# Earlier raw weight loads, an output weight in quarters, and a third projection bank in a hybrid decoder layer

## The chip, the core and the metric

The kernel runs on one core of a Trainium2 chip. A core has a matrix engine (TensorE, PE in the profile), a vector engine (VectorE, DVE), a scalar engine (ScalarE, ACT), GpSimd (POOL) and SyncE (SP), which here issues all DMA transfers. The engines run side by side, each through its own instructions in order, and wait for one another by semaphores. The metric is the device time of one execution in microseconds (us), the median of several runs.

## What is computed

One decoder layer for 1024 tokens of width 1024, in float32. Cut to what matters here:

```python
u = rmsnorm(h, mix_pre_norm)
z = u @ w_in                                   # 48 column tiles of 128
o_attn = dilated_attention_branch(z_attn)      # three groups, rotary q and k
o_rwkv = rwkv7_time_mix(z_rwkv, ...)           # a delta-rule recurrence over the tokens
gate_attn, gate_rwkv = split(sigmoid(z_gate))
merged = gate_attn * (o_attn @ w_attn_up) + gate_rwkv * (o_rwkv @ w_rwkv_up)
h = h + rmsnorm(merged @ w_out, mix_post_norm)
f = square(relu(rmsnorm(h, ffn_pre_norm) @ w_ff_in)) @ w_ff_out
h = h + rmsnorm(f, ffn_post_norm)
h = h + rmsnorm((p @ w_ple) * sigmoid(h @ w_ple_gate), ple_post_norm)
```

Every large product is made of three matmuls on operands that are split into a high and a low part (hi x hi, hi x lo, lo x hi; lines 310, 312 and 314).

## The kernel before

**Order.** The program is written out by a planner (`Order`, line 141) that keeps a clock `sch.t` of its own, an estimate of where PE stands. Two kinds of work are mixed. *Chains* are generators for everything with dependencies (the RWKV recurrence, attention, evacuations); each says when it wants to go on. The *dense list* (`dense`) holds large matmul tiles that fill PE while the chains wait. An entry has a gate (a condition), a load and a body. `pick` (line 186) takes the first entry whose gate is open; an entry without a gate is taken only when it is first. `fill` (line 197) starts a tile; before it goes on, it runs every *job* that is still pending and then calls `ahead`, which picks the following tile and issues its load. So a tile's weight is fetched while the tile before it runs.

**Jobs.** `soon(t, job)` (line 175) puts a job off to the planner's estimate of a landing, plus 0.2 us. The split of a raw weight into high and low part is such a job.

**Weights.** `wload` (line 331) takes a raw tile `wr` of 128 x 1024, starts its DMA (512 KB), and splits it: ACT copies it to `wh`, POOL subtracts twice to get `wl`. `wr`, `wh` and `wl` have two buffers each. The loads of the RWKV output (`load_or`, line 271) and the quarters of the output weight (`wsplit`, line 341) use the same two `wr` buffers.

**Who keeps whose order.** PE runs in written order throughout. While the recurrence runs (until the last `post` is done), ACT, DVE, POOL and SP do too. During attention only SP does; after it, in the merges, SP doesn't either, and the framework's scheduler orders these engines.

**Stages that matter here.** The projection tiles come in units: r, k and v for the recurrence (four units), then q, k and v for attention (six), with 16 gate tiles among and behind them. A tile has two halves of 24 matmuls of 512 tokens (`add_z`, line 490; `zhalf`, line 367). Each half fills one PSUM bank, taken by `zbank` (line 360) in turn from z0, z1 and, outside the recurrence, s0. The evacuation of a half of r, k or v is an ACT copy and a DVE operation that adds the token shift; of q or k an ACT copy, after the second half four DMA swaps of 32 rows (`sw`) and the rotary product on POOL and DVE.

In the recurrence, `invert` (line 708) solves the triangular blocks of one unit by 31 steps of small DVE operations and ends with transposes (line 739 is the first of these); `fold` (line 790) then combines the blocks. Its transposes "at" (line 801) and the scan (line 851) use the banks s0 and s1.

After attention come eight merges (`merge`, line 1282). Each loads its weight (384 KB) and two gate rows `g`, makes 24 matmuls from the RWKV output (`bk`) and 12 from the attention output (`z`), multiplies both by the gates on DVE, and splits the sum into `mt`. Merge 1 also fetches the first half of the output weight: `wo_half(0, GA)` at line 1301, four quarters of 512 KB, each split by ACT and DVE. The output projection (`out_0`, line 1366) reads it after merge 7.

Of the kernel before, what the change touches and what calls it, by code (L numbers as in the profile page):

```python
# [10 lines left out]
F32 = mybir.dt.float32  # L11
F32R = mybir.dt.float32r
AF = mybir.ActivationFunctionType
OP = mybir.AluOpType
# [12 lines left out]
NU = RW // 128  # L27
# [113 lines left out]
class Order:  # L141
# [4 lines left out]
    def __init__(self):  # L146
        self.t = self.dep = 0.0
        self.exact = False
        self.chains = []
        self.jobs = []  # L150
        self.dense = []
        self.cur = self.nxt = None
        self.busy = {}
        self.form = None
        self.held = None
        self.kept = []
        self.written = Written()
# [11 lines left out]
        self.chains.append([self.t + after, prio, gen])  # L169
        self.chains.sort(key=lambda c: c[1])  # L170

    def add(self, body, load=None, gate=None, late=False):
        self.dense.append((gate, load, body, late))

    def soon(self, t, job):

# [6 lines left out]
        self.jobs.append(jobs)  # L183
        self.spawn(due(), 0)

    def pick(self):
        for i, (gate, load, body, late) in enumerate(self.dense):
            if gate() if gate else i == 0:
                del self.dense[i]
                return body(*load()) if load else body(), late  # L190
        return None

    def ahead(self):
        if self.nxt is None:
# [23 lines left out]
        return d > 0  # L218

    def run(self):  # L220
        while self.chains or self.cur or self.dense or self.nxt:
            self.let_go(self.t)
            for c in self.chains:
                if c[0] <= self.t:
                    try:
                        self.dep = self.t
                        d = next(c[2])
                        c[0] = self.dep + LAG if d is None else self.t + d
                    except StopIteration:
                        self.chains.remove(c)  # L230
                    break
            else:
                if not self.fill():
                    self.t = max(self.t + 0.1, min((c[0] for c in self.chains), default=0.0))
                    assert self.t < 1e4
# [27 lines left out]
def layer(ctx: ExitStack, tc: tile.TileContext, x, pT, wz, wup, w_out, wff1, w_ff2, w_ple, w_pleg,  # L263
# [3 lines left out]
    sch = Order()  # L267
# [54 lines left out]
    def wait(cond):  # L322
        while not cond():
            yield 0.1
# [3 lines left out]
        yield from sch.free(tag)  # L328
        return psum.tile(shape, F32, name=name, tag=tag), tag

    def wload(src, n=1024):
        raw = wpool.tile([128, 1024], F32, name="wr")
        land = SY.dma_start(raw[:, :n], src)
        hi = wpool.tile([128, 1024], F32R, name="wh")
        lo = wpool.tile([128, 1024], F32R, name="wl")

        def split():
            S.activation(hi[:, :n], raw[:, :n], AF.Copy)
            for c in (slice(0, n // 2), slice(n // 2, n)):
                G.tensor_tensor(lo[:, c], raw[:, c], hi[:, c], OP.subtract)  # L340
        if ("X", 0) in done:
            sch.soon(land, split)
        else:
            split()
        return hi, lo
# [9 lines left out]
    upool = ust.enter_context(tc.tile_pool(name="u", bufs=1, side="right"))  # L355
    uT = [[upool.tile([128, KT, 512], F32R, name=f"u{p}{h}") for h in range(2)] for p in "hl"]

    zn = [0]

    def zbank():  # L360
        tags = ("z0", "z1", "s0")
        if ("X", 0) in done and ("P", NU - 1, 1) not in done:
            tags = tags[0:2]
        zn[0] += 1
        return psum.tile([128, 512], F32, name="z", tag=tags[zn[0] % len(tags)])

    def zhalf(ps, hi, lo, h):
# [122 lines left out]
    def add_z(wi, evac, gate=None):  # L490
        def body(hi, lo):
            for h in range(2):
                ps = zbank()
                yield from zhalf(ps, hi, lo, h)
                evac(h, ps)
                sch.let_go()
        sch.add(body, lambda: wload(wz[wi]), gate)

    def add_gate(j):
        def evac(h, ps):  # L500
# [207 lines left out]
    def invert(w):  # L708
# [29 lines left out]
        q, q2 = slice(0, 32), slice(32, 64)  # L738
        V.transpose(TN[q, :, q].rearrange("s q p -> s p q"), X[q].rearrange("q t p -> q p t"))
        d0 = V.end  # L740
        yield max(V.end - LEAD - sch.t, 0.0)
        V.transpose(TA[q2, :, :, q2].rearrange("p c h t -> p t c h"),
                    X[q2].rearrange("q t (c h) -> q t c h", h=2))
# [46 lines left out]
    def fold(w):  # L790
        d = U[w]
        AR, BK, TM, TN, UV, wc = (d[n] for n in ("AR", "BK", "TM", "TN", "UV", "wc"))
        for b in range(4):
# [3 lines left out]
            S.activation(TM[:, 4 * b:4 * b + 4, 0], ps.rearrange("p c (h k) -> p c h k", h=2), AF.Copy)  # L797
            sch.hold(tag)
        t0 = sch.dep
        for b in range(2):  # L800
            ps, tag = yield from chain_bank([128, 4, 128], "at", ("s0", "s1"))
            for i in range(4):
                c = 8 * b + 2 * i
                tr(ps[:, i, :], AR[:, 0, c:c + 2].rearrange("p c t -> p (c t)"), 0.11)
            for i in range(2):
                S.activation(BK[0:64, 8 * b + i:8 * b + 8:2, :], ps[64 * i:64 * i + 64], AF.Copy)
            sch.hold(tag)
# [472 lines left out]
        orT[w] = (hl[:, 0], hl[:, 1])  # L1280

    def merge(j):
        def load():
            hi, lo = wload(wup[j], 768)
            if j % 2 == 0:
                gt = [rtile([128, T], "g", t) for t in ("a", "kk")]
            else:
                gt2 = rtile([128, 2, T], "g", "BT")
                gt = [gt2[:, 0], gt2[:, 1]]
            for n in range(2):  # L1290
                land = SY.dma_start(gt[n], g_scr[2 * j + n])

            def gates():
                for g in gt:
                    S.activation(g, g, AF.Sigmoid)
            sch.soon(land, gates)
            return hi, lo, gt

        def body(hi, lo, gt):
            if j == 1:  # L1300
                wo[0] = wo_half(0, GA)
            ga, gr = gt
            wk = [(hi[:, i * 128:(i + 1) * 128], lo[:, i * 128:(i + 1) * 128]) for i in range(6)]
            def second(hs):
                ps = bank(("s1", "s2") if j < 2 else ("s1", "s2", "m0", "m1"))
                yield from mm3(ps, [wk[2 + i] + (orT[i][0][:, hs], orT[i][1][:, hs]) for i in range(NU)])
                V.tensor_tensor(gr[:, hs], gr[:, hs], ps, OP.mult)

            for hs in halves if j < 7 else ():
                yield from second(hs)  # L1310
            for h, hs in enumerate(halves):
                if j == 7:
                    yield from second(hs)
                while ("A", h) not in done or sch.t < OA_t[h]:
                    yield 0.0
                if mT[0][h] is None:
                    for p in range(2):
                        mT[p][h] = mtile("hl"[p], h, [128, KT, 512], f"mt{p}{h}", F32R)
                ps = zbank()
                yield from mm3(ps, [wk[i] + (oh[:, hs], ol[:, hs]) for i, (oh, ol) in enumerate(oaT)])  # L1320
                V.tensor_tensor(ga[:, hs], ga[:, hs], ps, OP.mult)
                V.tensor_tensor(ga[:, hs], ga[:, hs], gr[:, hs], OP.add)
                S.activation(mT[0][h][:, j, :], ga[:, hs], AF.Copy)
                V.tensor_tensor(mT[1][h][:, j, :], ga[:, hs], mT[0][h][:, j, :], OP.subtract)
        sch.add(body, load, lambda: ("B", 5) in done)

    for j in range(8):
        merge(j)
# [20 lines left out]
    def wo_half(c, tags):  # L1349
# [6 lines left out]
            res += [(hi[:, k, :], lo[:, k, :]) for k in range(2)]  # L1356
        return res

    def tok(i):
        return i // 4, slice((i % 4) * 128, (i % 4) * 128 + 128)  # L1360

    wo = {}
    y0 = {}
    ss0 = const.tile([128, 8], F32, name="ss0")

# [880 lines left out]
```

## Time and profile before

| | |
|---|---|
| median of 3 runs | 1735.56 us (1735.06 to 1738.82) |
| the profiled execution, its own time | 1735.81 us |
| its span, first to last instruction | 1733.8 us |
| mean granted clock of PE | 0.994 |
| HBM read, written | 196.50 MB, 81.79 MB |
| DMA issues of raw projection weights (`wr<-in_wz_dram`) | 48 of 512 KB, median 4.8 us to landing |

How to read the profile: a group is named by line, engine and operation, output <- inputs by the program's names. Operations that go through the planner's helper all have line 118, so the names tell them apart. In a timeline, a line gives start, duration, engine, line, operation, names, shape and count; in brackets stands the idle time of the engine just before, and what ended it. PE's matmuls overlap, so one shows some 0.39 us while they start about 0.23 us apart. The granted clock is a share of full speed. "SPq" are the DMA issues of SP; a transfer lands later.

### The profile page before, as it was taken

The numbers are of one execution on the slowest core, as the hardware profiler recorded it, in microseconds if no ns is written. First come the engines' busy times: TensorE is split into PE (matmuls) and PEld (weight loads), VectorE is DVE, ScalarE is ACT, GpSimd is POOL, SyncE is SP. The second block draws the span as 40 slices with busy tenths as digits, with TensorE's granted clock in tenths as the row PEclk, the third lists the DMA queues.
The fourth block names the chain that finished last, engine by engine and source line by source line (L and its number), as shares of the span: only waits on it lengthen the run. The fifth ranks groups of instructions, "written<-read, shape, count | busy, mean of one in ns | idle before, by whom it ended". The sixth has DMA issues, their size and how long they took to land.

```text
span 1733.8 us, 26821 instructions
## 1 busy us (share of the span) xinstructions
PE 1705.6 (98%) x10048; PEld 1394.3 (80%) x10048; DVE 1169.8 (67%) x2066; ACT 755.6 (44%) x1391; POOL 684.4 (39%) x491
## 2 busy tenths in 40 slices
PE   9999999999999999999899999999999999999998
PEld 8877888887887777776688888788888888888887
DVE  6377778677645666674664753688888888887644
ACT  5823334241425555444443465543443443443354
POOL 1222121120232323233240135877777777772311
PEclk9999999999999999999999999999999999999999
DMA  4621221221325866665642259466566566567611
GB/s 166 216 85 37 68 80 56 92 74 62 111 62 183 275 214 231 216 224 181 231 173 98 79 200 355 155 221 217 189 221 221 189 219 224 189 229 266 209 49 49
DMA packets 111491, 286.73 MB, mean 165 GB/s; under 512 B 12673, under 2 KB 13057, under 8 KB 110850
## 3 DMA queue, kind: packets, MB, share of 16 engines
q1 hardware_dynamic: 111362, 285.03, 47.7%
q8 instruction: 79, 1.29, 0.3%
q14 instruction: 50, 0.41, 0.1%
HBM read 196.50 MB, written 81.79 MB: 161 GB/s over the span
## 4 chain that ended last, share of the span: by engine, by line
PE 51%; DVE 2%; DMA 1%; ACT 1%; issue 1%; POOL 0%; SPq 0%; DVEq 0%; ACTq 0%; POOLq 0%
PE bk L314 9%; PE bk L310 9%; PE bk L312 9%; PE z L314 7%; PE z L310 7%; PE z L312 7%; PE tp L301 1%; DMA wr<-in_wz_dram 1%; DVE hh L118 0%; DMA wr<-in_w_out_dram 0%; ACT SB L118 0%; DMA g<-gscr 0%; PE cb L293 0%; DMA wr<-oscr 0%; DVE tot L118 0%
## 5 line engine op out<-in xcount | busy, mean ns | idle before, releaser
L118 POOL TENSOR_TENSOR wl<-wr,wh 128x512 fp32r<-128x512 f32 (+1 forms) x112 | 158.8, 1439 | 510.5 <-ACT wh L118 497.2
L310 PE MATMUL z<-uh,wh 128*128 128x512 f32 (+1 forms) x800 | 313.9, 392 | 6.6 <-DVE v L118 2.7
L314 PE MATMUL z<-uh,wl 128*128 128x512 f32 (+1 forms) x800 | 314.2, 393 | 1.8 <-POOL wl L118 1.8
L312 PE MATMUL z<-ul,wh 128*128 128x512 f32 (+1 forms) x800 | 313.0, 391 | 1.3 <-DVE ul L118 1.3
L118 DVE TENSOR_TENSOR tot<-tot,bk 128x512 f32<-128x512 f32 x417 | 273.0, 682 | 54.8 <-PE bk L314 54.7
L310 PEld LDWEIGHTS z<-uh,wh 128*128 128x128 f32 x800 | 151.6, 189 | 38.7 <-ACT wh L118 5.9
L314 PEld LDWEIGHTS z<-uh,wl 128*128 128x128 f32 x800 | 151.4, 189 | 34.2 <-issue 3.9
L312 PEld LDWEIGHTS z<-ul,wh 128*128 128x128 f32 x800 | 151.3, 189 | 31.4 <-issue 2.8
L310 PE MATMUL bk<-duo 128*128 128x512 f32 x420 | 163.5, 389 | 0.2 <-DVE hr L118 0.2
L314 PE MATMUL bk<-duo 128*128 128x512 f32 x420 | 163.4, 389 | 0.0
L312 PE MATMUL bk<-duo 128*128 128x512 f32 x420 | 163.4, 389 | 0.0
L118 ACT ACTIVATE wh<-wr 128x1024 fp32r<-128x1024 f32 (+2 forms) x94 | 81.0, 862 | 101.0 <-DMA wr<-in_wz_dram 46.6
L118 ACT ACTIVATE hr<-hr 128x512 f32<-128x512 f32 x96 | 60.7, 633 | 129.3 <-DVE hr L118 127.8
L118 POOL TENSOR_TENSOR duo<-sum,duo 128x512 fp32r<-128x512 f32 x60 | 84.1, 1401 | 51.5 <-ACT duo L118 51.5
L310 PEld LDWEIGHTS bk<-duo 128*128 128x128 f32 x420 | 78.8, 188 | 16.9 <-ACT wl L118 0.6
L312 PEld LDWEIGHTS bk<-duo 128*128 128x128 f32 x420 | 78.8, 188 | 16.4
L314 PEld LDWEIGHTS bk<-duo 128*128 128x128 f32 x420 | 78.8, 188 | 16.3
L118 DVE TENSOR_TENSOR hr<-hr,z 128x512 f32<-128x512 f32 x80 | 54.8, 685 | 52.2 <-PE z L314 50.5
L118 POOL TENSOR_TENSOR sw<-sw,rope 128x1024 f32<-128x1024 f32 x12 | 36.5, 3043 | 135.3 <-DMA sw<-qk 104.0
L118 ACT ACTIVATE duo<-sum 128x512 fp32r<-128x512 f32 x68 | 42.6, 628 | 108.1 <-DVE sum L118 106.4
L310 PE MATMUL z<-f,wh 128*128 128x512 f32 x212 | 82.6, 390 | 0.7 <-ACT pa L118 0.7
L312 PE MATMUL z<-f,wh 128*128 128x512 f32 x212 | 82.5, 389 | 0.0
(368 smaller groups left out, 3864.1 us busy)
## 6 DMA issues: line engine op xcount, KB each, us to landing
duo<-bs SPq DMA_DIRECT2D x60, 512.0 KB, 4.1
wr<-in_wz_dram SPq DMA_DIRECT2D x48, 512.0 KB, 4.8
bs<-OTB SPq DMA_DIRECT2D x35, 512.0 KB, 5.9
w2r<-in_w_ff_dram SPq DMA_DIRECT2D x32, 512.0 KB, 5.3
wr<-in_wff_dram SPq DMA_DIRECT2D x56, 256.0 KB, 3.6
w2e<-in_w_ff_dram SPq DMA_DIRECT2D x26, 512.0 KB, 6.1
bs<-duo SPq DMA_DIRECT2D x25, 512.0 KB, 6.4
hr<-p1scr SPq DMA_DIRECT2D x48, 256.0 KB, 3.1
```

The source lines that it names most:

```text
L118: return f(*a, **kw)
L301: PE.transpose(out_, a, ident if idn is None else idn)
L310: PE.matmul(ps, ah, bh, start=start and i == 0, stop=False, skip_group_check=not start)
L312: PE.matmul(ps, ah, bl, start=False, stop=False, skip_group_check=not start)
L314: PE.matmul(ps, al, bh, start=False, stop=i == n - 1, skip_group_check=not start)
```

## The change

Three edits in one.

1. *Raw weights half a tile sooner.* Entries of the dense list get a fifth field `raw`, a function that takes a raw tile and starts its DMA. After the first half of a projection tile (once the recurrence is over) and after the first half of a merge's second loop, `raw_ahead` looks at the dense list. If the first entry is the one that would be picked, has such a function, and no job is pending, it is taken off the list and its raw DMA is issued. The next `pick` then uses it: its split is put off to a landing that by then is near or past.
2. *The output weight's quarters.* `wo_half(0, GA)` in merge 1 becomes `wo_part(0)` to `wo_part(3)` in merges 1 to 4. Each fetches one quarter; its split is a job instead of being issued at once.
3. *A third projection bank up to the first fold.* `zbank` keeps s0 in turn until `invert` of the first unit has issued its first transpose ("fold"), instead of giving it up when the recurrence starts. `zin` holds the bank of the half that isn't evacuated yet; `fold` waits until that isn't s0 before it uses s0.

```diff
@@ class Order
-    def add(self, body, load=None, gate=None, late=False):
-        self.dense.append((gate, load, body, late))
+    def add(self, body, load=None, gate=None, late=False, raw=None):
+        self.dense.append((gate, load, body, late, raw))
...
+    def which(self):
+        return next((i for i, d in enumerate(self.dense) if (d[0]() if d[0] else i == 0)), None)
+
     def pick(self):
-        for i, (gate, load, body, late) in enumerate(self.dense):
-            if gate() if gate else i == 0:
-                del self.dense[i]
-                return body(*load()) if load else body(), late
-        return None
+        if self.raw:
+            (_, load, body, late, _), got = self.raw
+            self.raw = None
+            return body(*load(got)), late
+        i = self.which()
+        if i is None:
+            return None
+        _, load, body, late, raw = self.dense.pop(i)
+        return body(*(load(raw()) if raw else load())) if load else body(), late
+
+    def raw_ahead(self):
+        i = self.which()
+        if i == 0 and not self.raw and not any(self.jobs) and self.dense[i][4]:
+            d = self.dense.pop(i)
+            self.raw = d, d[4]()
...
-    def wload(src, n=1024):
+    def wraw(src, n=1024):
         raw = wpool.tile([128, 1024], F32, name="wr")
-        land = SY.dma_start(raw[:, :n], src)
+        return raw, SY.dma_start(raw[:, :n], src)
+
+    def wload(src, n=1024, got=None):
+        raw, land = got or wraw(src, n)
...
-    zn = [0]
+    zn, zin = [0], set()
 
     def zbank():
         tags = ("z0", "z1", "s0")
-        if ("X", 0) in done and ("P", NU - 1, 1) not in done:
+        if "fold" in done and ("P", NU - 1, 1) not in done:
             tags = tags[0:2]
         zn[0] += 1
+        zin.clear()
+        zin.add(tags[zn[0] % len(tags)])
...
@@ add_z, body
                 evac(h, ps)
+                zin.clear()
                 sch.let_go()
-        sch.add(body, lambda: wload(wz[wi]), gate)
+                if h == 0 and ("P", NU - 1, 1) in done:
+                    sch.raw_ahead()
+        sch.add(body, lambda got: wload(wz[wi], got=got), gate, raw=lambda: wraw(wz[wi]))
@@ invert, after the first transpose to TN
+        done.add("fold")
@@ fold, before the transposes "at"
+        yield from wait(lambda: "s0" not in zin)
@@ merge
-        def load():
-            hi, lo = wload(wup[j], 768)
+        def load(got):
+            hi, lo = wload(wup[j], 768, got)
...
-            if j == 1:
-                wo[0] = wo_half(0, GA)
+            if j in (1, 2, 3, 4):
+                wo_part(j - 1)
...
+                if h == 0:
+                    sch.raw_ahead()
-        sch.add(body, load, lambda: ("B", 5) in done)
+        sch.add(body, load, lambda: ("B", 5) in done, raw=lambda: wraw(wup[j], 768))
...
+    def wo_part(i):
+        if i == 0:
+            parts[:] = pieces(GA, "wo0", F32R)
+            wo[0] = []
+        raw = wpool.tile([128, 1024], F32, name="wr")
+        land = SY.dma_start(k2(raw), w_out[256 * i:256 * i + 256, halves[0]].rearrange("(k p) c -> p k c", p=128))
+        hi, lo = parts[i], parts[4 + i]
+
+        def split():
+            S.activation(hi, raw, AF.Copy)
+            V.tensor_tensor(lo, raw, hi, OP.subtract)
+        sch.soon(land, split)
+        wo[0] += [(k2(hi)[:, k, :], k2(lo)[:, k, :]) for k in range(2)]
```

More of the change, by code (lines that the diff above doesn't have):

```diff
@@ L151, in __init__ @@
         self.dense = []
-        self.cur = self.nxt = None
+        self.cur = self.nxt = self.raw = None
         self.busy = {}
@@ L220, in run @@
     def run(self):
-        while self.chains or self.cur or self.dense or self.nxt:
+        while self.chains or self.cur or self.dense or self.nxt or self.raw:
             self.let_go(self.t)
@@ L1357, in wo_half @@
         return res
+    def wo_part(i):
[10 more added lines that the diff above has]
+        wo[0] += [(k2(hi)[:, k, :], k2(lo)[:, k, :]) for k in range(2)]
     def tok(i):
         return i // 4, slice((i % 4) * 128, (i % 4) * 128 + 128)
-    wo = {}
+    wo, parts = {}, []
     y0 = {}
```

## The prediction

> **What bounds the kernel now.** I read the page first. TensorE (PE) sets the time, and none of the changed lines removes a matmul.
>
> ```profile
> span 1733.8 us, 26821 instructions
> ...
> PE 1705.6 (98%) x10048; PEld 1394.3 (80%) x10048; DVE 1169.8 (67%) x2066; ACT 755.6 (44%) x1391; POOL 684.4 (39%) x491
> ```
>
> PE is idle for 1733.8 - 1705.6 = 28.2 us. No edit can gain much more than those gaps and whatever else they cost. The waits of PE come next: who ended its idle time, total, times, longest.
>
> ```profile
> PE bk L310 <- ACT wh L118: 5.6, 1, 5.6
> PE z L310 <- DVE v L118: 2.7, 1, 2.7
> PE z L310 <- ACT wh L118: 2.0, 1, 2.0
> ...
> PE pt L301 <- ACT SB L118: 1.3, 2, 0.9
> ...
> PE rc L301 <- DVE row L118: 1.1, 1, 1.1
> ```
>
> The first three stand out, and each belongs to one part of the change. To see whether a gap costs more than its idle time, I asked for windows behind each and two undisturbed ones (columns: window, its length, busy time of the five engines, granted PE clock, DMA share, GB/s).
>
> ```profile
> 148.00:154.00 6.00, 4.35 (x12) 3.51 (x13) 5.93 (x11) 0.64 (x1) 3.66 (x3) 0.72 0.00 0
> 612.00:622.00 10.00, 8.46 (x30) 6.04 (x31) 6.24 (x15) 6.12 (x16) 2.95 (x2) 0.66 0.66 240
> 852.00:858.00 6.00, 4.83 (x14) 3.44 (x15) 1.53 (x3) 3.27 (x5) 3.46 (x4) 0.63 0.62 221
> 863.00:896.00 33.00, 33.00 (x147) 27.35 (x146) 23.49 (x32) 14.84 (x20) 11.54 (x9) 1.00 0.46 162
> ...
> 1200.00:1250.00 50.00, 50.00 (x222) 41.42 (x221) 42.65 (x61) 17.31 (x30) 39.67 (x30) 1.00 0.63 213
> ```
>
> Behind each gap the clock falls, while an undisturbed stretch of merges has 1.00. The lost clock is 6 x 0.28 = 1.68 us in the first window. In the second it is 10 x 0.34 = 3.4, less some 0.1 that falls on idle time, so 3.3. In the third it is 6 x 0.37 = 2.22, less half of the 1.17 us that were idle, so 1.63. The gaps therefore cost their idle time and 6.6 us more.
>
> [...]
>
> **Part by part: the third projection bank.** Each projection half (24 matmuls) fills one PSUM bank. With two banks, a half waits for the evacuation of the half two before it.
>
> ```profile
> 95.23 0.47 PE L310 MATMUL z<-uh,wh 128*128 128x512 f32 x1 [0.70 <-ACT gst L118]
> 149.65 0.53 PE L310 MATMUL z<-uh,wh 128*128 128x512 f32 x1 [2.67 <-DVE v L118]
> ...
> 94.35 0.74 DVE L118 SCALAR_TENSOR_TENSOR v<-z,pr,v 128x511 f32<-128x511 f32 x1
> ...
> 148.77 0.73 DVE L118 SCALAR_TENSOR_TENSOR v<-z,pr,v 128x511 f32<-128x511 f32 x1
> ...
> 154.98 0.74 DVE L118 SCALAR_TENSOR_TENSOR v<-z,pr,v 128x511 f32<-128x511 f32 x1
> ```
>
> The second gap ends 0.15 us after the DVE operation on v is done (149.50); DVE sat in the inverse's many small operations. The first gap ends 0.14 us after the v operation at 94.35 (95.09), so I read it as the same wait although the row names gst. With three banks both halves find a bank that was emptied long before. What is late next: the half starts at 149.65 - 2.67 = 146.98 and takes 24 x 33.00 / 147 = 5.4 us. The next needs the bank freed at 149.50 and starts near 152.4; the one after it needs the bank freed at 155.72 and starts near 157.8. Neither waits. Gain: 0.70 + 2.67 + 1.68 = **5.05 us**.
>
> The edit adds a wait: the fold's transposes "at" stand back while a projection sits in s0. Behind them in the same chain are the scan and the read-out. By counting banks from the start (six taken before this stage, then two per tile), the half that DVE leaves in the row below is the 26th and the last in s0; the next goes to z1, used two halves earlier and free.
>
> ```profile
> 197.44 0.73 DVE L118 SCALAR_TENSOR_TENSOR k<-z,pr,k 128x511 f32<-128x511 f32 x1
> ...
> 198.23 1.04 PE L301 MATMUL at<-cs,AR 128*128 128x128 f32 x8
> ```
>
> DVE leaves that half's bank at 198.17, the transposes start at 198.23. With the 0.15 us hop seen above they are at most some 0.1 late. Bounds: nothing, and 0.7 us (the gap at 95.23) if the order shifts. I take 0.2, near the rows.
>
> **Raw weight half a tile sooner.** A tile's raw weight (512 KB) is fetched at the start of the tile before. There, SP has four swaps of q or k ahead of it, and these wait for the evacuation.
>
> ```profile
> 601.20 2.41 SPq L137 DMA_DIRECT2D sw<-qk  x4
> 603.71 0.53 SPq L137 DMA_DIRECT2D wr<-in_wz_dram  x1
> ...
> DMA to landing us min/median/max: 4.6/4.8/5.0
> ...
> 610.95 1.06 ACT L118 ACTIVATE v<-z 128x512 f32<-128x512 f32 x1 [3.89 <-PE z L314]
> 611.82 1.05 ACT L118 ACTIVATE wh<-wr 128x1024 fp32r<-128x1024 f32 x1
> ...
> 612.92 0.50 PE L310 MATMUL z<-uh,wh 128*128 128x512 f32 x1 [2.00 <-ACT wh L118]
> 614.27 0.79 PE L314 MATMUL z<-uh,wl 128*128 128x512 f32 x1 [0.62 <-POOL wl L118]
> ```
>
> The weight landed near 603.7 + 4.8 = 608.5, but ACT held its split behind v's evacuation, which waited for PE until 610.95. That is the gap of 2.00 + 0.62 us. Its neighbours' evacuations give the middles of tiles:
>
> ```profile
> 584.35 1.05 ACT L118 ACTIVATE qk<-z 128x512 f32<-128x512 f32 x1
> ...
> 593.23 1.09 ACT L118 ACTIVATE qk<-z 128x512 f32<-128x512 f32 x1 [3.06 <-PE z L314]
> ```
>
> Fetched at the middle of the k tile (593, ahead of the swaps), it lands near 598, its split is ordered at the start of the v tile, and PE finds it ready.
>
> The condition is that the tile is first in the list with its gate open, and that no split is pending. For this tile the gate is the end of the second unit's scores:
>
> ```profile
> 585.40 0.72 PE L293 MATMUL sc<-qk 64*128 64x128 f32 x8
> ```
>
> This is the fourth and last set of that unit, 8 us ahead of 593, and the split then pending should be ordered some 7.6 us into that tile (the planner's constants: 0.8 for the evacuation, five issues of 0.6, 3.6 to land, 0.2), whose first half takes 8.9 (584.35 to 593.23). It works from about 575 on and feeds itself: each early load leaves nothing pending at the next middle. Gain: 2.62 + 3.3 = 5.9. The last gate tile's 0.62 us has the same cause (its load sits in SP behind three loads of the RWKV output):
>
> ```profile
> 797.67 0.43 SPq L137 DMA_DIRECT2D wr<-in_wz_dram  x1
> ...
> 806.28 0.51 PE L314 MATMUL z<-uh,wl 128*128 128x512 f32 x1 [0.62 <-POOL wl L118]
> ```
>
> Together **6.5 us**. No DMA is added. Each moves past four swaps, the w2 loads and the stores queued in SP. The split moves ahead of exponentials on ACT and of the rotary product on POOL. ACT's and POOL's order is not written out by hand here, so a split may now delay something else: between nothing and a gap like that at 612 (2.62 + 3.3). A gain is possible too: the waits "pt" and "rc" of 2.4 us in all lie in this stage. I take 0.3 lost, the size of the smaller pt wait (1.3 - 0.9 = 0.4).
>
> **A quarter per merge.** Merge 1 now issues all four quarters of the output weight through the two raw buffers, between the raw weights of merges 2 and 3.
>
> ```profile
> 836.38 2.02 SPq L137 DMA_DIRECT2D wr<-in_w_out_dram  x2
> ...
> 843.78 2.35 DVE L118 TENSOR_TENSOR wo<-wr,wo 128x1024 fp32r<-128x1024 f32 x2
> ...
> 845.03 0.38 SPq L137 DMA_DIRECT2D wr<-in_w_out_dram  x1
> 846.16 0.33 SPq L137 DMA_DIRECT2D wr<-in_wup_dram  x1
> ...
> 852.04 0.83 ACT L118 ACTIVATE wh<-wr 128x768 fp32r<-128x768 f32 x1
> 852.92 0.80 PE L310 MATMUL bk<-orw,wh 128*128 128x512 f32 x1 [5.60 <-ACT wh L118]
> 854.39 0.79 PE L314 MATMUL bk<-orw,wl 128*128 128x512 f32 x1 [0.25 <-POOL wl L118]
> ```
>
> Merge 3's weight goes out at 846.16, when DVE has done the third quarter (843.78 + 2.35 = 846.13). That is too late by 5.60 + 0.25 us. In the new order the buffers alternate: weights of merges 2, 3, 4 in one, quarters in the other. Merge 3's weight then takes the buffer that the second quarter took at 836.38, and can go out when merge 1 is two thirds done. What is late next is the last quarter, in merge 4; the output projection reads it after merge 7. The quarters keep their four loads, four ACT copies and four DVE subtractions of 2.35 / 2 = 1.18 us each, one per merge. DVE has room: 23.5 of 33 us in the four later merges, 28.2 with four subtractions more. Gain: 5.85 + 1.63 = **7.5 us**.
>
> **Sum.** 5.05 + 6.5 + 7.5 = 19.05, less 0.5, gives 18.55. The profiled execution took 1735.81 (span 1733.8 and 2.0 around it), 0.25 above the median of 1735.56. From the median the forecast is **1717.0 us**. Later PE has no gap to take it back: the window from 1200 has 50.00 of 50.00 us busy.
>
> **Rivals.**
> 1. *The early load does not reach the tile at 612, or the new order of ACT opens one gap like it.* For: the condition on pending splits is met with some 2 us to spare, and this very gap came from ACT's order alone, the weight having landed 2 us earlier. Against: the middles before and after would also start the series. Price 2.62 + 3.3 = 5.9: 1723. Chance 0.19.
> 2. *The half clock isn't tied to gaps this short.* Then the 1.68 and 3.3 us stay: 1722. The windows speak against it. Chance 0.05. [...]
> 3. *Gaps move on.* Planner times of loads change; three gaps like that at 612 give 3 x 5.9 = 17.7 us back: 1734.7, no change. Chance 0.06.
> 4. *Slower: an early weight load holds SP.* SP issues in order here. If the load has no free raw buffer, the swaps behind it wait, and so do rotary and scores. The rows:
>
> ```profile
> 605.61 2.41 POOL L118 TENSOR_TENSOR sw<-sw,rope 128x1024 f32<-128x1024 f32 x1 [5.62 <-DMA sw<-qk]
> ...
> 615.42 1.65 PE L293 MATMUL sc<-qk 64*128 64x128 f32 x8
> ```
>
> Rotary ends at 608.0 and, with a DVE sum of 1.2 us, at about 609.3: 6.1 us of slack before the scores. A hold of 8.7 us opens a gap of 2.6 with 3.3 of half clock behind it; in all four units of the early load that is 23.6: 1740.6. It decides from a hold of 6.1 us. Against: the buffer was emptied a tile before. Chance 0.06.
>
> **How the numbers follow.** The forecast has 0.64. Changes below 0.2% (3.5 us) can't be told from none. Forecast and rivals 1 and 2 are faster: 0.88; rival 3 the same: 0.06; rival 4 slower: 0.06. The low end takes in the 2.4 us of short waits, the 0.5 of costs and a little clock: 1712.5, some 4.5 below the forecast. The high end takes rivals 1 and 2 with a few short waits: 1726. Outside lie rivals 3 and 4.
>
> **What would show it.** Right: PE waits without "bk <- ACT wh" and "z <- DVE v" of over 1 us, clock 1.00 from 100 to 950 us, raw loads issued ahead of the swaps, one w_out load per merge. Wrong: a PE wait on swaps or scores, on g in the merges, or on the bank s0 at the first fold; or a low clock without a gap ahead of it.

## The result, and the profile after

The changed kernel takes 1723.58 us (median of 4 runs, 1719.45 to 1726.14), the kernel before 1735.85 beside it: a ratio of 0.9924, with a 95% interval from 0.9901 to 0.9947. On a second chip (the first experiment below) it was 0.9950, from 0.9933 to 0.9967. The change is faster: the medians lie 12.3 us apart in the first measurement and 8.8 in the second; 18.55 were forecast. The profiled execution is the slowest of the four, 1726.14 us. Three single executions among the runs below (one in e2, one in e3, one of the kernel before beside e11) took 3655 to 4421 us and are left out of every median and ratio.

Its page, the span and the busy times (share of the span, number of instructions):

```profile
span 1724.4 us, 26810 instructions
...
PE 1704.6 (99%) x10048; PEld 1395.6 (81%) x10048; DVE 1172.8 (68%) x2066; ACT 755.4 (44%) x1391; POOL 684.3 (40%) x491
```

PE is idle for 1724.4 - 1704.6 = 19.8 us, against 1733.8 - 1705.6 = 28.2 before. The five gaps that the prediction names (0.70, 2.67, 2.62, 0.62, 5.85) make 12.46 us and are all gone; PE's idle time fell by only 8.4, so some 4 us of waits are new. The list of PE's waits in the changed kernel (waiting line, releaser, us in total, times, the longest) begins:

```profile
PE rc L314 <- DVE row L118: 1.8, 1, 1.8
PE bk L327 <- DVE mt L118: 1.3, 1, 1.3
PE bk L323 <- ACT wh L118: 1.3, 1, 1.3
...
PE cb L306 <- DVE row L118: 0.8, 1, 0.8
```

(Lines 323, 325 and 327 are 310, 312 and 314 of before.) Their places, from PE's timeline (start, duration, operation; idle time just before in brackets):

```profile
591.32 0.66 PE L314 MATMUL rc<-cs,row 8*128 8x8 f32 x8 [1.75 <-DVE row L118]
...
801.40 1.09 PE L306 MATMUL cb<-row,sel 64*128 64x512 f32 x3 [0.81 <-DVE row L118]
...
875.12 0.50 PE L323 MATMUL bk<-orw,wh 128*128 128x512 f32 x1 [1.32 <-ACT wh L118]
876.21 0.50 PE L327 MATMUL bk<-orw,wl 128*128 128x512 f32 x1 [0.35 <-POOL wl L118]
877.62 0.50 PE L327 MATMUL bk<-orw,wl 128*128 128x512 f32 x1 [0.45 <-POOL wl L118]
891.52 0.50 PE L327 MATMUL bk<-wo,mt 128*128 128x512 f32 x1 [1.34 <-DVE mt L118]
```

Two waits stand before small matmuls of attention's end. Four, 3.46 us in all, stand in the last merge and the first output tile: what the quarters won in merge 3 is given back there in good part.

The clock isn't 1.00 up to 950 either. Windows of 2 us (length, busy us of PE, PEld, DVE, ACT and POOL, granted clock, DMA share, GB/s):

```profile
592.00:594.00 2.00, 2.00 (x5) 1.59 (x6) 2.00 (x4) 0.63 (x1) 0.00 (x0) 0.52 0.96 377
594.00:596.00 2.00, 2.00 (x7) 1.57 (x6) 1.90 (x3) 0.00 (x0) 0.00 (x0) 0.62 0.81 223
...
802.00:804.00 2.00, 2.00 (x7) 1.12 (x6) 2.00 (x4) 1.85 (x3) 0.84 (x2) 0.93 0.22 90
804.00:806.00 2.00, 2.00 (x4) 0.92 (x5) 1.88 (x4) 1.84 (x3) 0.62 (x1) 0.50 0.00 0
806.00:808.00 2.00, 2.00 (x6) 1.52 (x6) 2.00 (x3) 0.01 (x1) 1.28 (x1) 0.50 0.94 292
808.00:810.00 2.00, 2.00 (x6) 1.56 (x5) 0.48 (x1) 0.63 (x1) 0.00 (x0) 0.50 0.61 232
810.00:812.00 2.00, 2.00 (x8) 1.16 (x6) 0.00 (x0) 0.00 (x0) 0.00 (x0) 0.86 0.00 0
```

The time lost is 2 us times what the clock lacks to 1: 0.96 + 0.76 = 1.72 us at 592, and 0.14 + 3 x 1.00 + 0.28 = 3.42 at 802. The first follows a wait of 1.75 us, the second one of only 0.81. PE counts as busy all through (2.00 of 2.00 us in each of these rows, at 0.50 too): the low clock makes no idle time there and is seen in the clock column alone. In the same way before loses 1.70 at 148, 3.42 at 614 and 3.42 at 848 (there a part runs inside the gap and costs nothing). All are multiples of 1.7: stretches of 3.4 us at half clock (0.50 in the rows above). The two spans differ by 9.4 us: 8.4 of idle time and 1.0 of busy time.

### The profile page after: what moved, and what is told of

It reads as the page before. It is cut to its first block, busy times and chain, and to the rows that moved or that the text cites. A ratio compares the mean times of both kernels' runs of the same rounds, so it can differ in the third digit from the quotient of the medians.

```text
span 1724.4 us, 26810 instructions
## 1 busy us (share of the span) xinstructions
PE 1704.6 (99%) x10048; PEld 1395.6 (81%) x10048; DVE 1172.8 (68%) x2066; ACT 755.4 (44%) x1391; POOL 684.3 (40%) x491
## 4 chain that ended last, share of the span: by engine, by line
PE 57%; DVE 2%; DMA 2%; ACT 1%; POOL 1%; issue 1%; DVEq 0%; ACTq 0%; POOLq 0%
PE z L323 9%; PE z L325 9%; PE z L327 9%; PE bk L323 8%; PE bk L327 8%; PE bk L325 8%; DMA wr<-in_w_out_dram 1%; PE tp L314 1%; DMA g<-gscr 1%; PE sc L306 1%; PE po L306 1%; POOL wl L118 1%; PE pt L314 1%; DVE hh L118 0%; ACT wh L118 0%
## 5 line engine op out<-in xcount | busy, mean ns | idle before, releaser
L323 PE MATMUL z<-f,wh 128*128 128x512 f32 x212 | 82.7, 390 | 0.7 <-ACT pa L118 0.7
L325 PE MATMUL z<-f,wh 128*128 128x512 f32 x212 | 82.6, 390 | 0.0
L327 PE MATMUL z<-f,wh 128*128 128x512 f32 x212 | 82.6, 389 | 0.0
```

What stands on the lines that cost most here:

```text
L323: PE.matmul(ps, ah, bh, start=start and i == 0, stop=False, skip_group_check=not start)
L325: PE.matmul(ps, ah, bl, start=False, stop=False, skip_group_check=not start)
L327: PE.matmul(ps, al, bh, start=False, stop=i == n - 1, skip_group_check=not start)
```

## The experiments

Three theories had to be settled. *Additive*: the three parts are worth what the sum gave them. *Loop*: the quarters are worth little, since the gap before merge 3 had only covered another limit of the merges. *Clock by chance*: a short gap brings a stretch of half clock or not, by the moment at which it falls, differently from one execution to the next. The rivals are told with each run.

All results; the gain is (1 - ratio) times the median of before measured beside it, in brackets with the ratio's 95% interval. "Idle" is the span less PE's busy time in the profile, "clock" what the windows of 2 us lose from 20 us on, up to the last 15 us of the span (a low clock there falls on no work of PE: in the changed kernel it comes after 1720, and PE is done before 1718):

| kernel | median, us | before, us | ratio | gain, us | idle | clock |
|---|---|---|---|---|---|---|
| before, its first profile | | 1735.85 | | | 28.2 | 8.5 |
| changed, its first profile | 1723.58 | 1735.85 | 0.9924 | 13.2 (9.2 to 17.2) | 19.8 | 5.1 |
| e0 changed, again | 1726.30 | 1735.14 | 0.9950 | 8.7 (5.7 to 11.6) | 19.9 | 3.4 |
| e1 bank alone | 1729.32 | 1735.14 | 0.9975 | 4.3 (2.3 to 6.6) | 24.2 | 3.4 |
| e2 early loads alone | 1730.07 | 1735.14 | 0.9972 | 4.9 (2.9 to 6.8) | 22.6 | 5.1 |
| e3 quarters alone | 1733.03 | 1735.14 | 0.9995 | 0.9 (-1.0 to 2.6) | 24.9 | 3.4 |
| e11 bank and early loads | 1729.66 | 1734.65 | 0.9955 | 7.8 (5.0 to 10.8) | 20.6 | 8.5 |
| e4 three gate buffers | 1725.77 | 1736.99 | 0.9936 | 11.1 (8.7 to 13.5) | 21.1 | 3.4 |
| e5 mt copied by DVE | 1730.19 | 1736.99 | 0.9957 | 7.5 (5.0 to 10.1) | 22.9 | 6.8 |
| e6 e4, rc and cb later | 1725.13 | 1736.99 | 0.9933 | 11.6 (8.9 to 14.2) | 21.0 | 1.7 |
| e8 SP in written order | 1722.50 | 1734.21 | 0.9935 | 11.3 (9.2 to 13.5) | 18.4 | 0 |
| e9 e8 and e4 together | 1717.04 | 1734.21 | 0.9905 | 16.5 (13.9 to 19.1) | 14.1 | 0 |

(Of the 8.5 in before, 1.9 fall on idle time, so that the work there loses the 6.6 of the prediction.)

### The changed kernel again (e0)

No edit.

> The changed kernel unaltered, for a second profile. Its waits come from the written order of the program, so both theories expect them again within 0.2 us: 1.75 at rc (about 591), 0.81 at cb (801), 1.32 + 0.35 + 0.45 + 1.34 in the last merge and the first output tile. Theory A (whether a gap under 2 us brings half clock depends on where it falls in a clock window that runs free of the program): the half-clock stretches at 592-596 and 804-810 are gone, shorter or elsewhere, and the times spread by about 1.7 us steps between 1719 and 1726. Theory B (the half clock belongs to these matmuls, 64-row cb and 8-row rc): the same two stretches, 5.1 us lost in both profiles.

The waits came again within 0.2 us at rc (1.7) and cb (0.9), and in the last merge and first output tile as 1.96 + 0.35 + 0.69 = 3.0. The half clock stayed at 590 (1.70) and was gone at 802; a new stretch of 1.70 followed the wait of 1.96 at 874. The times run from 1720.22 (mean granted clock 0.999) to 1728.78 (0.994): most of the spread of this kernel is the number of such stretches. This fits theory A and not a property of the cb products; the last experiments below settle it.

### One part at a time (e1, e2, e3) and two together (e11)

e1, e2 and e3 are the changed kernel less two of its three parts, e11 less the quarters. Less the bank (in e2 and e3):

```diff
-        if "fold" in done and ("P", NU - 1, 1) not in done:
+        if ("X", 0) in done and ("P", NU - 1, 1) not in done:
...
-        yield from wait(lambda: "s0" not in zin)
```

Less the early loads, in the projections and in the merges (e1 and e3):

```diff
-                if h == 0 and ("P", NU - 1, 1) in done:
-                    sch.raw_ahead()
...
-                if h == 0:
-                    sch.raw_ahead()
```

Less the quarters (e1, e2 and e11):

```diff
-            if j in (1, 2, 3, 4):
-                wo_part(j - 1)
+            if j == 1:
+                wo[0] = wo_half(0, GA)
```

> Only the third projection bank until the first fold; loads and quarters as before. My sum: 0.70 + 2.67 of idle and 1.68 of half clock go, less 0.2: 1735.85 - 4.85 = 1731.0; the gaps at 612 (2.62) and 853 (5.85) stay. Rival (the half clock is not tied to those gaps, or the time is lost again at the fold): 1732.7 or more, with a wait on s0 or a clock under 1.00 between 50 and 240.

> Only the early raw loads (projection tiles and merges); two banks in the recurrence, the four quarters in merge 1 as before. My sum: -6.5 + 0.3, so 1729.6, with the gap at 612 gone, the waits at 95 and 149 (0.70, 2.67) kept and the gap in merge 3 (5.85) kept or grown, since the early load asks for a buffer that a quarter holds. Rival: the wait of 1.75 at rc and that of 0.81 at cb, with half clock behind each, come with this part: then it gains 6.5 - 0.7 - 0.8 - 5.1 at worst, 1735.

> Only the quarters, one per merge; no early raw loads, two banks. My sum: the 5.85 before merge 3 and 1.63 of half clock go: 1728.4. Theory now: without that gap nothing lets ACT and the gate rows catch up, so the last merge and the first output tile wait 2 to 4 us as in the changed kernel: 1731 to 1732. Rival: those waits come from the early raw loads, and are not here: 1728.4.

> The changed kernel without the quarters (bank and early loads; four quarters in merge 1 as before). Bank alone gave -5.8 us and the early loads alone -5.1 beside the same runs of before. If the two add up: 10.9 us less than before. Theory: the wait of 1.75 us at rc with half clock behind it (3.4 together), which neither part shows alone, is here, and they give 7.5 to 8; a wait of about 3.4 us stays in the merges, as with the early loads alone. Rival: the wait at rc needs the quarters too, and is not here: 10 to 11 us less.

**Bank.** Both gaps are gone, the clock is 1.00 from 20 to 840 us, and the interval of the gain, 4.3 (2.3 to 6.6), holds the 4.85 of the sum. The gap before merge 3 stays (6.20). But look at 612 in this kernel. It is there, a few us earlier. PE's timeline in e1, and the windows of 2 us behind the gap:

```profile
607.83 0.50 PE L323 MATMUL z<-uh,wh 128*128 128x512 f32 x1 [2.00 <-ACT wh L118]
609.18 0.50 PE L327 MATMUL z<-uh,wl 128*128 128x512 f32 x1 [0.62 <-POOL wl L118]
```

```profile
610.00:612.00 2.00, 2.00 (x18) 1.62 (x19) 1.35 (x1) 0.56 (x2) 0.80 (x1) 1.00 0.64 262
612.00:614.00 2.00, 2.00 (x11) 1.63 (x10) 1.90 (x11) 1.56 (x4) 0.00 (x0) 1.00 0.49 195
```

The clock stays at 1.00. The same gap of 2.00 + 0.62 us was followed by two stretches in before, by one in e3 (616 to 620) and by none here.

**Early loads.** The gap at 612 is gone, those in the recurrence stay (1.45 and 2.67). The wait in the merges shrinks from 5.6 to 3.4, where I had expected it kept or grown. The interval of the gain, 4.9 (2.9 to 6.8), holds the 6.2. cb waits 1.1 us, without half clock, so that wait comes with this part, as the rival says; rc does not wait.

**Quarters.** The gap of 5.85 is gone, and 1.08 + 0.35 + 0.45 + 1.34 = 3.22 us of new waits stand in the last merge and the first output tile, with a stretch of half clock at 896. There is no early load in this kernel, so the new waits belong to the quarters: the rival falls. Of 7.5 us 0.9 are left (-1.0 to 2.6).

**Two together.** The wait at rc (1.67, and one stretch behind it) is here, so it doesn't need the quarters; neither part shows it alone. It is no fixed cost of the two either: in e8 and e9 below it is 0.39 and none. The gain of 7.8 us (5.0 to 10.8) is what the theory said, though the times alone would also bear the sum of 4.3 and 4.9. A wait of 2.78 + 0.41 + 0.45 stays in the merges. The 5.1 us of half clock between 458 and 470 are taken up at the end.

### What holds the merges (e4, e5, e8, e9)

With DVE at two thirds and POOL at 40%, why does the last merge wait for the split `wh` of a weight that was loaded long before? ACT's timeline in the changed kernel:

```profile
862.50 1.06 ACT L118 ACTIVATE g<-g 128x1024 f32<-128x1024 f32 x1 [5.97 <-DMA g<-gscr]
...
871.46 1.06 ACT L118 ACTIVATE g<-g 128x1024 f32<-128x1024 f32 x1 [5.18 <-DMA g<-gscr]
...
873.72 0.61 ACT L118 ACTIVATE mt<-g 128x512 fp32r<-128x512 f32 x1
874.24 0.83 ACT L118 ACTIVATE wh<-wr 128x768 fp32r<-128x768 f32 x1
```

ACT idles 5 to 7 us (7.00 before the next such row, at 882.59), and what it waits for is a gate row; the mt copies and the weight's split stand behind its sigmoid. SP's queue and POOL's timeline show why the row is late:

```profile
857.92 0.80 SPq L137 DMA_DIRECT2D g<-gscr  x2
866.39 0.38 SPq L137 DMA_DIRECT2D wr<-in_w_out_dram  x1
866.82 1.04 SPq L137 DMA_DIRECT2D g<-gscr  x2
877.59 0.38 SPq L137 DMA_DIRECT2D wr<-in_w_out_dram  x1
878.03 0.93 SPq L137 DMA_DIRECT2D g<-gscr  x2
```

```profile
864.37 1.99 POOL L118 TENSOR_TENSOR wl<-wr,wh 128x384 fp32r<-128x384 f32 x2 [7.63 <-ACT wh L118]
...
875.14 2.42 POOL L118 TENSOR_TENSOR wl<-wr,wh 128x384 fp32r<-128x384 f32 x2 [8.78 <-ACT wh L118]
```

Gate rows go out every 9 to 11 us, while a merge's 36 matmuls, 0.227 us apart, take PE 8.2. Two things could hold them. One: a pair of rows needs the buffer of the merge two before, which is free after that merge's last subtraction, which waits for the mt copy, which stands behind a sigmoid. Two: ahead of the rows stands a load for the *second* half of the output weight, which the scheduler has put there; it needs a raw buffer, and POOL frees that at 866.36 and 877.56, 0.03 us ahead of each such load. POOL's split in turn waits for ACT's. Either way it is a loop through SP, ACT and DVE or POOL. The edits:

```diff
 e4   -            if j % 2 == 0:
      +            if j % 3 == 0:
       ...
      -                gt2 = rtile([128, 2, T], "g", "BT")
      +                gt2 = rtile([128, 2, T], "g", ("BT", "BK2")[j % 3 - 1])
 e5   -                S.activation(mT[0][h][:, j, :], ga[:, hs], AF.Copy)
      +                V.tensor_copy(mT[0][h][:, j, :], ga[:, hs])
 e8   -        in_order.__exit__(None, None, None)
      +        gn["turn"] = in_order
       ...
                       wo[1] = wo_half(1, GB)
      +                gn.pop("turn").__exit__(None, None, None)
 e9   e4 and e8
```

> The changed kernel, its merges' gate rows in three buffers in turn instead of two. Theory (a loop: a merge's last subtraction frees the gate rows, these are loaded, ACT's sigmoid of them stands ahead of the next merge's mt copy, on which that merge's last subtraction waits): one more buffer opens the loop, ACT no longer idles 5 to 7 us for a gate row, and the PE waits between 870 and 895 (3.46 and 3.0 us in the two profiles) fall below 0.8 in all; 3 to 4 us faster than the changed kernel, ratio to before about 0.993. Rival (DVE and POOL splits of the quarters, or the late raw weights, set the pace): the waits stay within 0.5 us.

> The changed kernel, with the high part mt of a merge's sum copied by DVE instead of ACT (16 copies). Theory of the loop: it opens the same loop at its other link, since no mt copy stands behind a sigmoid any more; PE waits between 870 and 895 below 0.8 us although DVE gets 16 x 0.6 = 10 us more work. Rival (DVE sets the pace of the merges): the waits grow by several us.

> The changed kernel, two gate buffers, but SP keeps the written order through the merges: the loads of the output weight's second half come behind the last gate rows and no longer hold them (in the changed kernel one goes out at 866.39 and 877.59, each 0.03 us after POOL has split a merge's weight, and the gate rows 0.43 behind it). Theory now: two loops run side by side, one through the two gate buffers and the mt copies, one through the raw weight buffer and SP. Opening this one alone leaves the other: 2 to 3 us of PE waits between 860 and 895 stay, 1724 to 1726. Rival (the raw buffer and SP are the only loop): they fall below 0.8 us.

> Both: three gate buffers and SP in written order. Theory of two loops: only now the PE waits between 860 and 895 fall below 0.8 us in all (3.5 and 3.0 in the changed kernel, 3.8 with three buffers alone), and ACT no longer idles 5 to 7 us for gate rows: 3 us faster than the changed kernel, about 1722. Rival (ACT's order of the weight split is the cause by itself): 2 us or more of waits stay.

PE's waits between 830 and 900 us, summed from the timelines:

| | load of the second half ahead of the rows | behind them (SP in written order) |
|---|---|---|
| two gate buffers | 3.46 and 3.0 (changed kernel), 3.2 (e3) | 1.75 (e8) |
| three gate buffers | 3.83 (e4) | none (e9) |

The first theory, that the gate buffers are the loop, fell with e4: the waits stayed. (Its ratio of 0.9936 is near the 0.993 that was expected; as the waits are still there, that is luck.) In its trace the rows still follow such a load, and that follows POOL (867.30 + 2.42 = 869.72). POOL, then SP in e4:

```profile
867.30 2.42 POOL L118 TENSOR_TENSOR wl<-wr,wh 128x384 fp32r<-128x384 f32 x2 [8.59 <-ACT wh L118]
```

```profile
869.75 0.38 SPq L137 DMA_DIRECT2D wr<-in_w_out_dram  x1
870.18 0.93 SPq L137 DMA_DIRECT2D g<-gscr  x2
```

e5 fell too: with mt on DVE the waits grew to 5.1 us (1.22 + 0.65 + 0.37 at 858, 1.92 + 0.96 at 892), and a load at 867.47 held the rows to 867.94. e8, with that load behind the rows, halves the waits: 1.75 us stay over all merges, where I had expected 2 to 3. Only 0.64 of them lie between 860 and 895, the stretch that the expectation named, so by its words the rival, that SP is the only loop, would have won. But the trace of e8 shows the second loop. There each pair of gate rows goes out 0.03 to 0.04 us after a merge's last subtraction on DVE (862.20 + 0.68 = 862.88), and SP, with the next weights behind the rows, waits for such subtractions 41.1 us in all between 822 and 885, against 4.3 in the changed kernel. DVE, then SP in e8:

```profile
862.20 0.68 DVE L118 TENSOR_TENSOR mt<-g,mt 128x512 fp32r<-128x512 f32 x1
```

```profile
862.91 0.80 SPq L137 DMA_DIRECT2D g<-gscr  x2
```

e9, with both opened, has no PE wait left. So there are two loops side by side. Opening the load on SP alone halves the waits, opening the buffers alone gives nothing, and only both together free PE. ACT still idles 3.9 to 5.6 us a merge ahead of gate rows in e9 (5 to 7 in the changed kernel): that idle time alone costs PE nothing. The window from 790 to 900 us in the changed kernel and in e9:

```profile
790.00:900.00 110.00, 105.63 (x438) 81.90 (x437) 70.81 (x94) 51.65 (x69) 41.64 (x29) 0.97 0.57 198
```

```profile
790.00:900.00 110.00, 109.25 (x471) 86.28 (x470) 74.73 (x96) 50.94 (x71) 38.18 (x28) 1.00 0.56 198
```

PE does 33 matmuls more in the same 110 us, 7.5 us at 0.227 each. About half of that is the merges': 3.4 us are the half clock behind cb, from 804 to 810, which the changed kernel's first profile had and its repeat had not. DVE does more work, not less: it was never the bound. e9 is the fastest kernel of all, 0.9905 (0.9890 to 0.9920); the interval of e0 begins above it, that of the first measurement overlaps it. Not all of its gain is the merges': the wait at rc is gone in e9 and 0.39 in e8 without an edit there. In the changed kernel a DVE sum lies ahead of the copy that rc waits for, and takes 2.85 us beside POOL's product (586.56 to 588.95); in e9 it takes 0.69, just ahead of POOL's. DVE in the changed kernel, then in e9:

```profile
586.64 2.85 DVE L1828 TENSOR_TENSOR OTB<-sum,OTB 128x512 fp32r<-128x512 f32 x1
589.42 1.84 DVE L118 COPY row<-rw 8x512 f32<-8x512 f32 x2
```

```profile
585.91 0.69 DVE L1829 TENSOR_TENSOR OTB<-sum,OTB 128x512 fp32r<-128x512 f32 x1
586.51 1.91 DVE L118 COPY row<-rw 8x512 f32<-8x512 f32 x2
```

### Ordering rc and cb later (e6)

To e4, ahead of rc, and with 1.5 for 2.0 ahead of cb:

```diff
-        yield None
+        yield sch.until(sch.dep + 2.0)
```

> As e4, and the transposes rc and the products cb are ordered 2.0 and 1.5 us later in PE's program, behind more of the dense tile. Waits of 1.75 and 0.8 gone as well, and with them what triggers the half clock at 590-596 and 802-812: clock of the runs 0.999, and 1726.3 - 3.2 - 2.6 - 3.4 = 1717. Rival (the half clock comes with the short cb and rc matmuls, not with the waits): the two stretches stay, 1720.5.

The waits moved and did not go. rc waits 0.6 and cb not at all, but scores now wait 1.6 us for rotary, and attention's output, now later, is waited for by merges: 0.94 us at 819, and then 2.58 at 854 for a gate product on DVE. No half clock is left at 590 and 802; one stretch of 1.70 us follows the wait of 2.58. The clock is better, 0.997 to 0.998 in every run, and the time is that of e4 (0.9933 and 0.9936). The forecast of 1717 failed.

### What a gap costs in clock (e7, e10)

Into the second MLP matrix, where PE has no gaps, waits of chosen length are put:

```diff
             if i in FIRST:
-                chain[t] = bank(XB)
+                prev, chain[t] = chain[3], bank(XB)
+                if t == 0 and x in (0, 4) and prev is not None:
+                    hops = 1 + gaps[0] % 6
+                    gaps[0] += 1
+                    g = [small.tile([128, 1], F32, name="gap", bufs=1) for _ in range(1)][0]
+                    S.activation(g, prev[:, 0:1], AF.Copy)
+                    for k in range(hops - 1):
+                        if k % 2:
+                            S.activation(g, g, AF.Copy)
+                        else:
+                            V.tensor_copy(g, g)
+                    PE.matmul(chain[t][0:1, 0:1], g, one1, start=True, stop=True)
```

In e10 `x == 0` and `hops = 6 + gaps[0] * 3 % 8`. The waits make both kernels slower (1842.35 us, a ratio of 1.0608, and 1787.14 us, 1.0304); only their profiles matter here.

> The changed kernel with 30 PE waits put into the stage from 1200 to 1700 us, where PE otherwise has none and its clock is 1.00: at every third and fourth product of the second MLP matrix a one-element matmul waits for a chain of 1 to 6 small copies on ACT and DVE that starts from the product before. Waits of about 0.5 to 3 us. Theory A (a gap brings half clock by chance, the more often the longer it is, in stretches of 3.4 us that lose 1.7 each): none or few of the waits under 0.8 us, about half of those at 1.5, nearly all over 2.5 are followed by a 2-us window under 1.00. [...]

> As e7, with 14 waits of lengths between: chains of 6 to 13 copies at every seventh product. From e7 (0 of 15 at 0.3 to 1.2 us, 14 of 15 at 3.1 to 4.0) I expect waits of 1.4 to 2.9 us. If half clock comes by chance with the length: roughly a quarter of those below 2 us and three quarters of those above are followed by it, each time in one or two stretches of 3.4 us. If there is a limit: none below it, all above.

One gap of e10 on PE's timeline, and the windows around it:

```profile
1386.67 0.19 PE L1972 MATMUL bk<-cs,gap 128*1 128x1 f32 x2 [2.53 <-ACT gap L118]
```

```profile
1384.00:1386.00 2.00, 0.14 (x1) 0.00 (x0) 0.91 (x5) 1.08 (x6) 2.00 (x3) 1.00 0.50 199
1386.00:1388.00 2.00, 1.33 (x5) 1.07 (x6) 0.15 (x1) 0.39 (x2) 1.05 (x1) 0.75 0.52 171
1388.00:1390.00 2.00, 2.00 (x6) 1.54 (x5) 1.10 (x2) 0.00 (x0) 0.00 (x0) 0.50 0.90 251
1390.00:1392.00 2.00, 2.00 (x9) 1.61 (x9) 1.54 (x3) 0.12 (x1) 0.00 (x0) 0.90 0.27 102
```

Read over all 43 gaps of the two profiles (29 and 14):

| gap, us | followed by half clock | stretches |
|---|---|---|
| 0.31 to 1.18 | 0 of 14 | |
| 1.37 to 1.87 | 2 of 5 | one each |
| 2.10 to 2.29 | 2 of 4 | one each |
| 2.53 to 2.95 | 5 of 5 | one each |
| 3.08 to 3.97 | 13 of 15 | 6 times one, 7 times two |

Seen by its length alone, a gap brings half clock by a chance that rises from none up to 1.2 us to nearly certain from 2.5 on, and each stretch loses 1.70 to 1.72 us (less where PE still waits in part of it). No single limit of the length shows: two gaps of the same 2.10 us came out differently:

```profile
1166.65 0.19 PE L1972 MATMUL bk<-cs,gap 128*1 128x1 f32 x2 [2.10 <-ACT gap L118]
...
1458.33 0.19 PE L1972 MATMUL bk<-cs,gap 128*1 128x1 f32 x2 [2.10 <-ACT gap L118]
```

The windows of 2 us behind the first have 1.00, those from 1458 on 0.67, 0.50 and 0.98. The last three mean half clock from 1458.68 to 1462.08. Worked out in this way, the starts and ends of all stretches of one profile lie on one grid with a step of 3.413 us: in e10 the starts 1240.24, 1458.68 and 1605.46 are 11, 75 and 118 steps behind the first, 1202.68 (402.78 / 118 = 3.413), and in e7 the starts 1155.40 and 1677.64 are 153 steps apart (522.24 / 153 = 3.413). Counted from the start of the span, the grid lies elsewhere from profile to profile: its first line at 3.1 us in before, 1.6 in the changed kernel, 0.1 in e1, 1.7 in e7 and 1.2 in e10. It tells the two gaps apart: the second has all of its 2.10 us in one cell of the grid, of the first 0.59 lie in one cell and 1.51 in the next. In the cells of e7 and e10 that had full clock, idle time of up to 1.62 us never brought half clock, 1.99 and more always did (20 cells), and between them two of four did (1.68 and 1.81, but not 1.84 and 1.94). So what looks like chance is mostly where the gap falls on a grid whose place differs from profile to profile. Outside this stage the limit is less sharp: 1.94 us of idle in a cell brought no half clock in the merges of e1, nor did 1.32 and 1.43 at the end of those of the changed kernel, but its wait of 0.81 us at cb, all in one cell, was followed by two stretches: something else takes part there.

## Why the prediction was right, and where it was wrong

**Right**: the sign, and the time inside its range (1712.5 to 1726.0). The third bank and the early loads did what the steps said: both gaps of the recurrence, that at 612 and that of the last gate tile are gone, no wait appears at the first fold or on swaps, and an early load holds SP for 0.7 us at most between 580 and 740 (rival 4 needed 6.1). Alone they measured 4.3 and 4.9 us against 4.85 and 6.2, both within the intervals. The range held in part by luck. Its high end was drawn for rivals 1 and 2, and the time came near the 1723 of rival 1, but the early load did reach the tile at 612, and what was lost was the quarters' gain, which no rival priced. The repeat's 1726.30 lies just outside.

**Wrong: the quarters.** The step that failed reads "DVE has room: 23.5 of 33 us in the four later merges" and "What is late next is the last quarter". DVE did have room, and the last quarter was not late. I summed busy time and did not follow what the merges wait for in a circle. Late next was the gate row, held on SP behind a load for the output weight's second half and, at the same time, by its own two buffers: a loop of 9 to 11 us per merge against PE's 8.2. The gap of 5.85 in merge 3 had hidden it. In before too such a load goes out at 878.36, 0.03 after POOL's split (875.88 + 2.45 = 878.33), but PE, held back by 5.85 us in merge 3, was not yet there to wait. POOL, then SP in before:

```profile
875.88 2.45 POOL L118 TENSOR_TENSOR wl<-wr,wh 128x384 fp32r<-128x384 f32 x2 [8.78 <-ACT wh L118]
```

```profile
878.36 0.38 SPq L137 DMA_DIRECT2D wr<-in_w_out_dram  x1
878.83 0.42 SPq L137 DMA_DIRECT2D g<-gscr  x1
```

Of 7.5 us 0.9 were left (e3, -1.0 to 2.6); in e9 no wait is left in the merges. The prediction named gate rows as what a wrong outcome would show, and gave it no price.

**Wrong in size: the clock.** I took 1.68 + 3.3 + 1.63 = 6.6 us of half clock as belonging to three gaps and as gone with them. The price of a gap depends on where it falls on the grid: the gap at 612 had two stretches in before, one in e3, none in e1. And the new waits of 1.75 to 1.96 us bring stretches of their own. The two profiles of the changed kernel still lose 5.1 and 3.4. The second rival, that half clock isn't tied to such short gaps, was rightly held unlikely (5 of 5 gaps of 2.53 to 2.95 us brought it), though e1 has the 2.00 + 0.62 us without it.

**Wrong in size: the scheduler's new order.** I took 0.3 us; rc and cb wait 1.75 + 0.81 where before waited 1.06 at another rc. The idle time lies inside the bound that I gave, a gap like that at 612 (2.62 + 3.3 = 5.92). With the half clock behind them the two waits cost 2.56 + 1.72 + 3.42 = 7.7 us in the first profile, which is outside, and 4.3 in the second.

In the profile's own terms: forecast 11.96 us of idle and 6.6 of clock; found 8.4 of idle and, in these two profiles, 1.5 of clock (6.6 - 5.1). That makes 9.9 for spans that differ by 9.4.

## What to carry to other kernels

When a stall is removed, ask not only which engine has room but which circle of waits (buffer, queue, copy, buffer) has a period longer than the tile's work: a stall upstream may have covered it. An engine that idles in each period can point at it, but proves nothing: ACT idles here with the loops closed (5 to 7 us a merge) and with both open (3.9 to 5.6). If one link is opened and nothing moves, look for a second circle through the same instruction before dropping the theory. And price a gap of the matrix engine with what may follow it: in e7 and e10, between full-size matmuls, that was nothing more up to 1.2 us (0 of 14 gaps), 1.7 us more in about half of the cases near 2 (4 of 9), once or twice 1.7 from 2.5 on (18 of 20); and compare such kernels over several runs, since the place of the grid differed from profile to profile.

## What the runs showed of the hardware

Half clock (0.50) comes in stretches of 3.4 us, one or several: 3.4 at 592 and twice that at 803.7 to 810.6 in the changed kernel. They lie on a grid with a step of 3.413 us, whose place differs from profile to profile (e7 and e10 above). The losses of 1.70 to 1.72 us are half of that step. Of the 14 gaps between 1.37 and 2.95 us in e7 and e10, 9 were followed by half clock.

A long idle time isn't needed for it. In e11 PE's timeline and its windows show

```profile
456.63 2.18 PE L306 MATMUL tq<-TN,TM 32*32 32x32 f32 x64 [0.15 <-DVE TN L118]
```

```profile
458.00:460.00 2.00, 2.00 (x31) 1.75 (x29) 1.97 (x2) 1.55 (x3) 0.00 (x0) 0.92 0.30 111
460.00:462.00 2.00, 2.00 (x12) 1.17 (x11) 2.00 (x2) 0.06 (x1) 0.00 (x0) 0.50 0.69 199
462.00:464.00 2.00, 2.00 (x42) 2.00 (x40) 0.63 (x1) 0.41 (x1) 0.00 (x0) 0.50 0.93 258
```

Three stretches (to 470, 5.1 us) follow 64 matmuls of 32 x 32 with a wait of 0.15 us; at the same matmuls the other profiles of this kernel and its variants had none. Two stretches each also follow the 64-row cb products (0.81 us of wait in the changed kernel, 1.18 in e4). But in before and in the changed kernel five groups of 64 matmuls of 32 x 32 (from 273.76, 375.23 and 382.35; from 268.37 and 377.07) lie whole within one cell of the grid, as the group of e11 does, and none of the five brought half clock. So such matmuls alone don't do it; what did stays open.
